# Gates from float32 one-hots with one product a token, and three more gathered rows in flight

## The chip, the cores and the metric

The kernel runs on one core of one Trainium2 chip. The metric is device time in microseconds (us) from launch to end, the median of several runs. Engines are named as in the profile: PE (TensorE matmul; PEld its weight loads), DVE (VectorE), ACT (ScalarE), POOL (GpSimd), SP (SyncE, which issues most DMAs here).

## The reference, cut to what matters

Two layers of a decoder over 512 tokens of width 1024. Each layer is a token mixer (two kinds of attention) with a norm, then a product-key expert layer ("PEER") with a norm. The expert layer is what the change touches:

```
scores = q . sub_keys                 # 8 heads, two halves of 128 keys
top 16 of each half -> sums -> top 16 of the sums:  idx (expert number, 0..16383), gate = softmax
u = expert_u[idx]; act = gelu(h . u)            # 128 selected experts a token, float32
v = expert_v[idx]; y = sum over selected of (gate * act) * v
```

So every token picks 128 of 16384 experts, each with a row of 1024 float32 in `expert_u` and one in `expert_v`.

## The kernel before, in words

The 512 tokens are four blocks of 128. Blocks 0 and 1 (`BLK_A`) take the rows of their experts by **gathering**: `gathers` (L611) fetches, for each of the 128 picks of a token, one row per token with an indirect DMA on POOL's queue (L624, 128 rows of 4 KB at a time), and DVE multiplies and sums it against h (L634, first 128 fetches, from `expert_u`) or adds it, weighted, to y (L643/L645, the next 128, from `expert_v`). A fetch lands in a tile of the pool `gat` (5 buffers of 4 KB a partition), and POOL may issue a fetch when a buffer of that pool is free, that is when DVE is done with an older row. There are 256 fetches for a block and 1024 in all; the four blocks of two layers take turns, one after the other.

Blocks 2 and 3 (`BLK_B`) are **dense**: `dense` (L754) multiplies h with all experts, in 32 chunks of 512 columns, weights the result with a dense matrix of gates, and multiplies that with `expert_v`. Weights stream from HBM; most products are made from high and low parts split by ACT (L748) and DVE (L750). Seven chunks (L776) may be computed before the gates are there; everything else of `dense` waits for the gates of both blocks (`yield f"gates {l} {b}"`).

`gates` (L657) makes that dense matrix and writes it to DRAM (`gdram`). It first calls `select` (L541), the top-16 search on DVE (with products on POOL, L582). Then expert number e is split into i = e >> 7 and j = e & 127, these and the gate are transposed so that a partition holds one of the 128 picks and a column one token (L675), and for each token the matrix G[j, i] = sum over picks of onehot_j x (onehot_i x gate) is one PE product. This goes in 32 steps of NT = 4 tokens a block. A step of the kernel before has, in bfloat16:

- two one-hots of 512 elements (`hots`, L688): on DVE as one comparison against `iota_b` (L700), or on ACT in five instructions (L696, L698)
- the gate is held as three bfloat16 parts that sum to it exactly, so there are three weighted one-hots (L711 on POOL or DVE, L709 on ACT in four instructions)
- `products` (L717): for each token three accumulating matmuls 128x128x128 (L723), and two ACT copies out of PSUM (L727) into a staging tile, which SP writes to DRAM every 32 tokens (L731).

Which engine makes a one-hot or a weighted one is the choice of `pick`, which takes the engine that would end first by a plan kept in the program: `free` holds the planned time at which each engine is next free, and each step tells its planned cost before it emits its instructions (`yield cost(lat=0.7, ACT=0.55, PE=0.8)` for a step of gates, to which `pick` adds; `pace` for a fetched row: DVE 1.14 or 1.2, POOL 1.04, DMA 1.46). All parts of the kernel are generators of that kind, and `run_threads` (L110) runs next the one that the plan can start first (a few us of lead decide between near ones). A step's planned start becomes the priority of its instructions; the framework then orders each engine's queue by priority among what its own timeline holds ready, and adds all waits. On the chip each queue runs in that fixed order.

Tiles of 2 KB a partition come from the pool `d2p` (18 buffers): the one-hots and weights of gates, but also tiles of attention (L270 to L273, L322), of `select`, of the query products (L510) and the split halves of `weigh` (L806, L807). Two more constants matter: `iota_b` holds 0..127 four times over, in bfloat16.

Of the kernel before, what the change touches and what calls it, by code (L numbers as in the profile page):

```python
# [18 lines left out]
P = 128  # L19
# [16 lines left out]
# Pairs (a, b) of ranks that can be among the 16 best sums: (a + 1) * (b + 1) <= 16.  # L36
ROWS = [(0, 1, 16), (1, 1, 8), (2, 1, 5), (3, 1, 4), (4, 1, 3), (5, 3, 2), (8, 8, 1)]
NCAND = sum(n * m for _, n, m in ROWS)
# Token blocks whose experts are gathered row by row (A); the others (B) go through
# products with all experts, in chunks of EC, weighted by a dense matrix of gates.  # L40
BLK_A = [0, 1]
BLK_B = [2, 3]
EC = 512
# [9 lines left out]
def trunk(ctx: ExitStack, tc: tile.TileContext, x, w_in, lam, subln_g, w_o, ln1, ln2,  # L53
# [10 lines left out]
    gat = ctx.enter_context(tc.tile_pool(name="gat", bufs=5))  # L64
    d2p = ctx.enter_context(tc.tile_pool(name="d2p", bufs=18))
# [26 lines left out]
    # The order of the instructions. Threads are generators that tell, before each step that  # L92
    # they emit, how long it will hold the engines; the step that can start first is next.
# [7 lines left out]
    def pick(**engines):  # L101
        """The engine that would end a piece of work first."""
        eng = min(engines, key=lambda e: free[e] + engines[e])
        free[eng] += engines[eng]
        return eng
# [33 lines left out]
    # constants  # L139
    ident = const.tile([P, P], F32, name="ident")  # L140
    make_identity(nc, ident)
    # minus the distance of a query from a key; no weight where the key is later
# [18 lines left out]
    iota_b = const.tile([P, P, NT], BF16, name="iota_b")  # L161
    nc.gpsimd.iota(iota_b, pattern=[[1, P], [0, NT]], base=0, channel_multiplier=0,
# [4 lines left out]
    hs = {}          # a block's h: an SBUF tile (A) or an AP in DRAM (B)  # L167
# [7 lines left out]
    def load_h(b):  # L175
        """A block's h in SBUF, in a tile that may be overwritten."""
        if b in on_chip:
            return hs[b]
        t = hap.tile([P, D], F32, name="ha") if b in BLK_A else t4()
        nc.sync.dma_start(t, hs[b])  # L180
        if b in BLK_A:
            hs[b] = t
            on_chip.add(b)
        return t
# [32 lines left out]
    def layer_params(l):  # L217
        p = {}
        lamt = a2()[:, :4 * HD].rearrange("p (a b) -> p a b", a=4)
        nc.sync.dma_start(lamt.rearrange("p a b -> p (a b)"), rows(lam[l], 4 * HD))  # L220
        tmp = a2()
        s2 = sml.tile([P, 2], F32, name="lam_s")
        for i in range(2):
            nc.vector.scalar_tensor_tensor(tmp[:, :HD], lamt[:, 2 * i, :], 1.0, lamt[:, 2 * i + 1, :],
                                           op0=ALU.mult, op1=ALU.mult, accum_out=s2[:, i:i + 1])
        e2 = sml.tile([P, 2], F32, name="lam_e")
        nc.scalar.activation(e2, s2, AF.Exp)
        li = 0.8 - 0.6 * math.exp(-0.3 * l)
        p["nlam"] = prm.tile([P, 1], F32, name="nlam")
        # -(e1 - e2 + li)  # L230
        nc.vector.scalar_tensor_tensor(p["nlam"], e2[:, 1:2], -li, e2[:, 0:1],
                                       op0=ALU.add, op1=ALU.subtract)
        p["sub_g"] = prm.tile([P, VD], F32, name="sub_g")
        nc.sync.dma_start(p["sub_g"], rows(subln_g[l], VD))
        nc.vector.tensor_scalar_mul(p["sub_g"], p["sub_g"], 1.0 - li)
        LP[l] = p
# [12 lines left out]
    def pipeline(items, stages, skew, c):  # L249
        """Emits the stages of each item, stage k of an item skew[k] steps behind its first."""  # L250
        n = len(items)
        state = [None] * n
        for i in range(n + skew[-1]):
            yield c
            for k, stage in sorted(zip(skew, stages), key=lambda x: -x[0]):
                if 0 <= i - k < n:
                    state[i - k] = stage(items[i - k], state[i - k])

    def attention(l, b, q, mixT):
        """mixT[feature, t] of a block from its queries and all keys up to it."""  # L260
# [135 lines left out]
        # heads of one parity share a tile: the others' keys lie on other partitions  # L396
# [17 lines left out]
    def mixer(l, blks, order, tails):  # L414
        """Token mixer and first norm of some blocks, and their queries and key scores."""
# [9 lines left out]
        # dq dk dv sq sk sv  # L425
        for n, key in ((1, "dk"), (2, "dv"), (0, "dq"), (4, "sk"), (5, "sv"), (3, "sq")):
            o = int(key[0] == "s")
            for b in blks:
# [12 lines left out]
                else:  # L441
# [6 lines left out]
                    else:  # L448
                        # scores in units of the head's slope, a power of two
# [18 lines left out]
    def mixer_out(l, tail, hq):  # L468
# [49 lines left out]
        for b in tail:  # L518
            if b in BLK_B:
                # exact parts of h for the products with all experts  # L520
                HT[b] = hq[b][0]
                xlo, xhi = HQ[b] = [fold(t4(F32R), DC) for _ in range(2)]
                nc.scalar.activation(xhi, hq[b][0], AF.Copy)
                nc.vector.tensor_tensor(xlo, hq[b][0], xhi.bitcast(F32), op=ALU.subtract)
            done[f"scores {l} {b}"] = clock[0]

    def best16(rows, val, pos):
        """The 16 largest of each row, and their positions; the rows are overwritten."""
# [12 lines left out]
    def select(l, b, half, idf, gate):  # L541
        """Expert numbers (as floats) and gates of half of a block's heads: [t, head, rank]."""
# [31 lines left out]
        for h in range(HH + 1):  # L574
            yield cost(DVE=1.35, POOL=1.9)
            if h < HH:
                # a one at the position of each rank, times the expert's number
# [33 lines left out]
    def gathers(l, b):  # L611
        """y = sum over the selected experts of gate * gelu(h . u) * v, rows gathered."""
# [44 lines left out]
    def gates(l, b):  # L657
        """Dense gates of a block to DRAM: gdram[l][j, t // GT, i, t % GT] of expert i * 128 + j."""
# [7 lines left out]
        yield cost(lat=3.0, DVE=2.0, PE=0.7)  # L666
# [9 lines left out]
        t0, t1 = a2(), a2()  # L676
        gp, ij = fold(t0[:, :3 * P], 3), fold(t0[:, 3 * P:].bitcast(BF16), 2)
        ijf, gb = fold(t1[:, :2 * P], 2), fold(t1[:, 2 * P:2 * P + 3 * P // 2].bitcast(BF16), 3)
        nc.vector.tensor_copy(ij.rearrange("p a t -> p (a t)"), pt[:, 0:2 * P])
        nc.scalar.copy(ijf.rearrange("p a t -> p (a t)"), pt[:, 0:2 * P])  # L680
        # three parts of a gate, exact in bfloat16
        nc.vector.tensor_copy(gp[:, 0, :], pt[:, 2 * P:3 * P])
        for k in range(3):
            nc.vector.tensor_copy(gb[:, k, :], gp[:, k, :])
            if k < 2:
                nc.vector.tensor_sub(gp[:, k + 1, :], gp[:, k, :], gb[:, k, :])
                nc.vector.tensor_copy(gp[:, k, :], gb[:, k, :])
        shp = [P, P, NT]  # L688

        def hots(tg, t0):  # L690
            t = tg * GT + t0
            hot = a2h().rearrange("p (a j t) -> p a j t", a=2, t=NT)
            for n in range(2):
                if pick(ACT=1.7, DVE=0.34) == "ACT":
                    for k in range(NT):
                        nc.scalar.activation(hot[:, n, :, k], iota_b[:, :, k], AF.Abs, scale=-1.0,  # L696
                                             bias=ijf[:, n, t + k:t + k + 1])
                    nc.scalar.activation(hot[:, n], hot[:, n], AF.Relu, scale=-1.0, bias=1.0)  # L698
                else:
                    nc.vector.tensor_tensor(hot[:, n], iota_b, ij[:, n, t:t + NT].unsqueeze(1).to_broadcast(shp),  # L700
                                            op=ALU.is_equal)
            w01 = a2h().rearrange("p (a j t) -> p a j t", a=2, t=NT)
            w2 = a2h()[:, :P * NT].rearrange("p (j t) -> p j t", t=NT)
            ws = (w01[:, 0], w01[:, 1], w2)
            for k, w in enumerate(ws):
                eng = pick(ACT=1.2, POOL=1.0, DVE=0.34)
                if eng == "ACT":
                    for n in range(NT):
                        nc.scalar.activation(w[:, :, n], hot[:, 0, :, n], AF.Copy, scale=gp[:, k, t + n:t + n + 1])  # L709
                else:  # L710
                    (nc.gpsimd if eng == "POOL" else nc.vector).tensor_tensor(  # L711
                        w, hot[:, 0], gb[:, k, t:t + NT].unsqueeze(1).to_broadcast(shp), op=ALU.mult)
            return hot, ws
# [3 lines left out]
        def products(tg, t0, hot, ws):  # L717
# [3 lines left out]
            for n in range(NT):  # L721
                for k, w in enumerate(ws):
                    nc.tensor.matmul(ps[:, n * P:(n + 1) * P], lhsT=hot[:, 1, :, n], rhs=w[:, :, n],  # L723
                                     start=(k == 0), stop=(k == 2))
# [10 lines left out]
        for t in range(0, P, NT):  # L735
            yield cost(lat=0.7, ACT=0.55, PE=0.8)
            todo.append((t // GT, t % GT, *hots(t // GT, t % GT)))
# [5 lines left out]
    def split(raw):  # L743
        """Exact halves, hi and lo, of a tile's two parts."""
# [9 lines left out]
    def dense(l):  # L754
        """y of the B blocks from products with all experts."""
# [4 lines left out]
        def first(ec):  # L760
            """gelu(h . u) of a chunk."""
# [29 lines left out]
        def weigh(ec):  # L791
            """Transposed, times the gates, in exact halves."""
# [124 lines left out]
```

## Time and profile before

| | us |
|---|---|
| median of 3 runs (3537.52 to 3541.9) | 3537.8 |
| span of the profiled execution, first to last instruction | 3535.5 |
| DVE busy | 2937.8 (83%) |
| PE busy | 2765.6 (78%) |
| POOL busy | 1681.0 (48%) |
| ACT busy | 1184.8 (34%) |
| DMA, mean rate | 292 GB/s |

No time of the profiled execution other than its span is shown; the median of the runs is 2.3 us above that span. Busy times are unions of an engine's instructions. The stretches of a layer can be told by the lines that run in them. In layer 0: projections until some 300 us; attention of blocks 1 to 3 until some 500; then selections, the gates of block 2 (608 to 784), the query products of blocks 1 and 3, the gates of block 3 (956 to 1089), and from 1110 to 1821 the dense products. Layer 1 repeats this with its gates at 2364 to 2533 and 2703 to 2837, and dense products from 2850 to 3513. The gathered rows run beside all of it, from 167 to 1767 and from 1904 to 3519.

### The profile page before, as it was taken

The numbers are of one execution on the slowest core, as the hardware profiler recorded it, in microseconds if no ns is written. First come the engines' busy times: TensorE is split into PE (matmuls) and PEld (weight loads), VectorE is DVE, ScalarE is ACT, GpSimd is POOL, SyncE is SP. The second block draws the span as 40 slices with busy tenths as digits, with TensorE's granted clock in tenths as the row PEclk, the third lists the DMA queues.
The fourth block names the chain that finished last, engine by engine and source line by source line (L and its number), as shares of the span: only waits on it lengthen the run. The fifth ranks groups of instructions, "written<-read, shape, count | busy, mean of one in ns | idle before, by whom it ended". The sixth has DMA issues, their size and how long they took to land.

```text
span 3535.5 us, 42200 instructions
## 1 busy us (share of the span) xinstructions
PE 2765.6 (78%) x14604; PEld 2214.2 (63%) x14604; DVE 2937.8 (83%) x5537; ACT 1184.8 (34%) x1900; POOL 1681.0 (48%) x1297
## 2 busy tenths in 40 slices
PE   7996474468576999999997876834694679999997
PEld 5776462366245888888776764613652468888885
DVE  2577889989998888888668678999799987888888
ACT  2114640411133444444231138404110434444442
POOL 0265645763675433334314655457536743344443
PEclk9997587579777999999998886865796689999998
DMA  5698796686769999999966987955966799999996
GB/s 228 212 329 294 246 333 201 206 302 231 261 222 360 360 347 343 349 351 348 369 222 253 331 286 237 351 177 196 337 220 232 256 367 343 349 346 354 345 344 251
DMA packets 283926, 1032.89 MB, mean 292 GB/s; under 512 B 25152, under 2 KB 91200, under 8 KB 231488
## 3 DMA queue, kind: packets, MB, share of 16 engines
q0 software_dynamic: 147456, 536.94, 42.4%
q1 hardware_dynamic: 136256, 493.26, 37.6%
q8 instruction: 115, 1.88, 0.2%
q14 instruction: 99, 0.81, 0.1%
HBM read 991.30 MB, written 38.80 MB: 291 GB/s over the span
## 4 chain that ended last, share of the span: by engine, by line
PE 40%; DVE 14%; issue 6%; DMA 5%; POOL 2%; ACT 2%; POOLq 0%; DVEq 0%; ACTq 0%
PE ps L822 7%; PE ps L821 7%; PE ps L824 6%; PE ps L786 5%; PE ps L785 5%; PE ps L784 5%; DVE row L634 3%; DMA row<-u,idx 2%; DVE ha L645 2%; POOL row L624 2%; DMA row<-v,idx 2%; PE ps L800 1%; DVE d L711 1%; DVE idf L586 1%; DVE d L579 1%
## 5 line engine op out<-in xcount | busy, mean ns | idle before, releaser
L624 POOL DMA_INDIRECT row<-v,idx x512 | 669.3, 1307 | 892.6 <-DVE ha L645 662.5
L624 POOL DMA_INDIRECT row<-u,idx x512 | 655.2, 1280 | 589.1 <-DVE row L634 375.9
L634 DVE SCALAR_TENSOR_TENSOR row<-row,ha 128x1024 f32<-128x1024 f32 x512 | 666.6, 1315 | 121.0 <-DMA row<-u,idx 118.1
L645 DVE SCALAR_TENSOR_TENSOR ha<-row,c,ha 128x1024 f32<-128x1024 f32 x508 | 700.3, 1379 | 58.0 <-DMA row<-v,idx 53.9
L750 DVE TENSOR_TENSOR t<-st,t 128x1024 fp32r<-128x1024 f32 x449 | 533.2, 1224 | 210.8 <-ACT t L748 210.7
L748 ACT ACTIVATE t<-st 128x1024 fp32r<-128x1024 f32 x456 | 453.9, 1056 | 36.6 <-PE ps L824 15.8
L723 PE MATMUL ps<-d,d 128*128 128x128 bf16 x1536 | 218.4, 295 | 207.0 <-DVE d L711 128.8
L821 PE MATMUL ps<-t,d 128*128 128x512 f32 x1024 | 314.2, 398 | 44.5 <-ACT d L806 44.5
L822 PE MATMUL ps<-t,d 128*128 128x512 f32 x1024 | 342.3, 395 | 0.0
L723 PEld LDWEIGHTS <-d 128*128 128x128 bf16 x1536 | 178.6, 121 | 234.5 <-issue 192.5
L824 PE MATMUL ps<-t,d 128*128 128x512 f32 x1024 | 316.7, 390 | 0.0
L785 PE MATMUL ps<-t,t 128*128 128x512 f32 x800 | 311.5, 389 | 0.5 <-DVE t L750 0.5
L786 PE MATMUL ps<-t,t 128*128 128x512 f32 x800 | 311.7, 390 | 0.0
L784 PE MATMUL ps<-t,t 128*128 128x512 f32 x800 | 304.2, 389 | 1.0 <-ACT t L748 1.0
L507 PE MATMUL ps<-t,st 128*128 128x128 f32 x2048 | 263.2, 293 | 35.2 <-DMA st<-w_query 35.2
L507 PEld LDWEIGHTS ps<-t,st 128*128 128x128 f32 x2048 | 257.8, 209 | 41.5 <-issue 29.5
L444 PE MATMUL ps<-t,st 128*128 128x128 f32 x2048 | 243.0, 281 | 22.2 <-ACT t L191 16.2
L444 PEld LDWEIGHTS ps<-t,st 128*128 128x128 f32 x2048 | 238.9, 197 | 28.6 <-ACT t L191 18.6
L821 PEld LDWEIGHTS ps<-t,d 128*128 128x128 f32 x1024 | 190.4, 190 | 82.4 <-ACT d L806 45.5
L822 PEld LDWEIGHTS ps<-t,d 128*128 128x128 f32 x1024 | 190.1, 190 | 47.0 <-DVE t L750 10.2
L824 PEld LDWEIGHTS ps<-t,d 128*128 128x128 f32 x1024 | 192.2, 188 | 40.9 <-DVE d L807 0.3
L806 ACT ACTIVATE d<-t 128x512 fp32r<-128x512 f32 x128 | 78.7, 632 | 410.9 <-DVE t L803 410.9
(175 smaller groups left out, 4190.8 us busy)
## 6 DMA issues: line engine op xcount, KB each, us to landing
st<-ut SPq DMA_DIRECT2D x128, 1024.0 KB
st<-vd SPq DMA_DIRECT2D x128, 1024.0 KB
st<-w_in SPq DMA_DIRECT2D x48, 1024.0 KB
st<-w_query SPq DMA_DIRECT2D x48, 1024.0 KB
gd<-st SPq DMA_DIRECT2D x32, 1024.0 KB
t<-gd SPq DMA_DIRECT2D x64, 512.0 KB
st<-w_o SPq DMA_DIRECT2D x24, 1024.0 KB
ln<-ln SPq DMA_DIRECT2D x16, 512.0 KB
```

Source lines behind the costliest of these rows:

```text
L444: nc.tensor.matmul(ps[:, f * P:(f + 1) * P], lhsT=w(c, slice(f * P, (f + 1) * P)), rhs=hT[:, c, :], start=(c == 0), stop=(c == DC - 1))
L507: nc.tensor.matmul(ps[:, f * P:(f + 1) * P], lhsT=w(c, slice(f * P, (f + 1) * P)), rhs=hq[b][0][:, c, :], start=(c == 0), stop=(c == DC - 1))
L624: nc.gpsimd.indirect_dma_start(out=g, out_offset=None, in_=src, in_offset=bass.IndirectOffsetOnAxis(ap=idx[s // (NSEL // 2)][:, s % (NSEL ...
L634: nc.vector.scalar_tensor_tensor(g, g, 1.0, h1, op0=ALU.mult, op1=ALU.mult, accum_out=c[:, s:s + 1])
L645: nc.vector.scalar_tensor_tensor(y, g, c[:, s:s + 1], y, op0=ALU.mult, op1=ALU.add)
L750: (nc.gpsimd if eng == "POOL" else nc.vector).tensor_tensor(lo, part, hi.bitcast(F32), op=ALU.subtract)
L784: nc.tensor.matmul(ap[b], lhsT=xhi, rhs=hi[:, c, :], start=(d == 0), stop=False)
L785: nc.tensor.matmul(ap[b], lhsT=xhi, rhs=lo[:, c, :], start=False, stop=False)
L786: nc.tensor.matmul(ap[b], lhsT=xlo, rhs=hi[:, c, :], start=False, stop=(d == DC - 1))
L821: nc.tensor.matmul(y[b][n], lhsT=shi, rhs=hi[:, n, :], start=start, stop=False)
L822: nc.tensor.matmul(y[b][n], lhsT=shi, rhs=lo[:, n, :], start=False, stop=False)
L824: nc.tensor.matmul(y[b][n], lhsT=slo, rhs=hi[:, n, :], start=False, stop=stop)
```

## The change

`gates` makes float32 one-hots, all on DVE, one instruction for one token and one one-hot, and one product a token; the gate is no longer split. `d2p` goes from 18 to 14 buffers, `gat` from 5 to 8. Comments are dropped too. The core of the diff:

```diff
-    gat = ctx.enter_context(tc.tile_pool(name="gat", bufs=5))
-    d2p = ctx.enter_context(tc.tile_pool(name="d2p", bufs=18))
+    gat = ctx.enter_context(tc.tile_pool(name="gat", bufs=8))
+    d2p = ctx.enter_context(tc.tile_pool(name="d2p", bufs=14))
...
-    iota_b = const.tile([P, P, NT], BF16, name="iota_b")
-    nc.gpsimd.iota(iota_b, pattern=[[1, P], [0, NT]], base=0, channel_multiplier=0,
+    iota_b = const.tile([P, P], F32, name="iota_b")
+    nc.gpsimd.iota(iota_b, pattern=[[1, P]], base=0, channel_multiplier=0,
...
-        yield cost(lat=3.0, DVE=2.0, PE=0.7)
+        yield cost(lat=3.0, DVE=1.2, PE=0.7, ACT=0.4)
...
-        t0, t1 = a2(), a2()
-        gp, ij = fold(t0[:, :3 * P], 3), fold(t0[:, 3 * P:].bitcast(BF16), 2)
-        ijf, gb = fold(t1[:, :2 * P], 2), fold(t1[:, 2 * P:2 * P + 3 * P // 2].bitcast(BF16), 3)
-        nc.vector.tensor_copy(ij.rearrange("p a t -> p (a t)"), pt[:, 0:2 * P])
-        nc.scalar.copy(ijf.rearrange("p a t -> p (a t)"), pt[:, 0:2 * P])
-        nc.vector.tensor_copy(gp[:, 0, :], pt[:, 2 * P:3 * P])
-        for k in range(3):
-            nc.vector.tensor_copy(gb[:, k, :], gp[:, k, :])
-            if k < 2:
-                nc.vector.tensor_sub(gp[:, k + 1, :], gp[:, k, :], gb[:, k, :])
-                nc.vector.tensor_copy(gp[:, k, :], gb[:, k, :])
...
+        ijg = fold(a2()[:, :3 * P], 3)
+        nc.scalar.copy(ijg.rearrange("p a t -> p (a t)"), pt[:, :3 * P])
+
+        def hots(t):
+            hot, w = (fold(a2(), NT) for _ in range(2))
+            for k in range(NT):
+                nc.vector.tensor_scalar(hot[:, k, :], iota_b, ijg[:, 1, t + k:t + k + 1], None, op0=ALU.is_equal)
+                nc.vector.tensor_scalar(w[:, k, :], iota_b, ijg[:, 0, t + k:t + k + 1],
+                                        ijg[:, 2, t + k:t + k + 1], op0=ALU.is_equal, op1=ALU.mult)
+            return hot, w
...
             for n in range(NT):
-                for k, w in enumerate(ws):
-                    nc.tensor.matmul(ps[:, n * P:(n + 1) * P], lhsT=hot[:, 1, :, n], rhs=w[:, :, n],
-                                     start=(k == 0), stop=(k == 2))
+                nc.tensor.matmul(ps[:, n * P:(n + 1) * P], lhsT=hot[:, n, :], rhs=w[:, n, :],
+                                 start=True, stop=True)
...
-            yield cost(lat=0.7, ACT=0.55, PE=0.8)
+            yield cost(lat=1.6, DVE=1.6, ACT=0.9, PE=1.0)
```

The old `hots`, with its two uses of `pick`, goes whole. The copies out of PSUM (L727) and the writes to DRAM (L731) stay.

## Rows read from the trace of the kernel before

**Rows 1.** Gates stretches: start:end, length, PE, PEld, DVE, ACT, POOL, clock, DMA, GB/s.
```profile
608.00:784.00 176.00, 95.22 (x618) 80.91 (x619) 162.10 (x183) 54.73 (x122) 127.41 (x107) 0.64 0.72 250
956.00:1089.00 133.00, 89.58 (x467) 62.01 (x467) 126.77 (x214) 45.41 (x95) 98.63 (x82) 0.69 0.71 252
2364.00:2533.00 169.00, 91.89 (x586) 76.99 (x587) 151.13 (x175) 53.37 (x121) 121.04 (x102) 0.62 0.71 244
2703.00:2837.00 134.00, 88.46 (x467) 61.33 (x467) 125.47 (x214) 44.97 (x95) 100.97 (x83) 0.71 0.70 250
```
**Rows 2.** The same view: between the gates of layer 0, and its dense stretch.
```profile
784.00:956.00 172.00, 119.12 (x539) 78.94 (x539) 164.02 (x583) 21.07 (x32) 76.28 (x59) 0.86 0.68 246
...
1110.00:1800.00 690.00, 683.68 (x3235) 562.97 (x3234) 559.07 (x624) 297.21 (x381) 266.74 (x183) 1.00 0.93 349
```
**Rows 3.** Groups of instructions, whole trace: the lines that go (busy, mean ns, idle before).
```profile
L700 DVE TENSOR_TENSOR d<-iota_b,d 128x512 bf16<-128x512 bf16 x245 | 130.2, 569 | 0.0
L711 DVE TENSOR_TENSOR d<-d,d 128x512 bf16<-128x512 bf16 x195 | 123.6, 662 | 0.1
L711 POOL TENSOR_TENSOR d<-d,d 128x512 bf16<-128x512 bf16 x166 | 196.7, 1197 | 26.8 <-DVE d L700 23.4 <-PE ps L776 1.1 <-PE ps L723 0.5
```
**Rows 4.** Groups of DVE, the gathered rows alone, in the four gates stretches in order.
```profile
L645 DVE SCALAR_TENSOR_TENSOR ha<-row,c,ha 128x1024 f32<-128x1024 f32 x62 | 100.1, 1615 | 13.8 <-DMA row<-v,idx 13.0 <-issue 0.2
...
L634 DVE SCALAR_TENSOR_TENSOR row<-row,ha 128x1024 f32<-128x1024 f32 x45 | 66.5, 1498 | 6.2 <-DMA row<-u,idx 6.2
...
L645 DVE SCALAR_TENSOR_TENSOR ha<-row,c,ha 128x1024 f32<-128x1024 f32 x55 | 90.6, 1647 | 17.9 <-DMA row<-v,idx 17.0
...
L634 DVE SCALAR_TENSOR_TENSOR row<-row,ha 128x1024 f32<-128x1024 f32 x45 | 64.6, 1458 | 8.5 <-DMA row<-u,idx 8.5
```
**Rows 5.** Instructions of one line, whole trace (ns min/median/max): rows and small DVE operations.
```profile
L645 DVE SCALAR_TENSOR_TENSOR ha<-row,c,ha x508: 1224/1280/4344, 455.9 to 3517.6; 128x1024 f32<-128x1024 f32 x170
L634 DVE SCALAR_TENSOR_TENSOR row<-row,ha x512: 1192/1219/7499, 167.5 to 3048.1; 128x1024 f32<-128x1024 f32 x171
L296 DVE TENSOR_SCALAR dg<-ident,rc x64: 260/280/471, 45.1 to 2212.3; 128x128 f32<-128x128 f32 x64
L643 DVE TENSOR_SCALAR ha<-row,c x4: 745/747/754, 453.6 to 3052.9; 128x1024 f32<-128x1024 f32 x4
L205 DVE TENSOR_SCALAR t<-t,ln_mv,ln_rs x8: 802/814/874, 477.2 to 3523.2; 128x1024 f32<-128x1024 f32 x8
```
**Rows 6.** Timeline of DVE, then of POOL, 2399 to 2405 (start us, us).
```profile
2399.79 4.88 DVE L205 TENSOR_SCALAR ha<-ha,ln_mv,ln_rs 128x1024 f32<-128x1024 f32 x1
...
2400.08 4.03 POOL L711 TENSOR_TENSOR d<-d,d 128x512 bf16<-128x512 bf16 x4
```
**Rows 7.** Timeline of DVE, then of POOL, 405.5 to 407.8.
```profile
406.86 0.28 DVE L296 TENSOR_SCALAR dg<-ident,rc 128x128 f32<-128x128 f32 x1
407.06 1.22 DVE L634 SCALAR_TENSOR_TENSOR row<-row,ha 128x1024 f32<-128x1024 f32 x1
...
405.97 1.51 POOL L624 DMA_INDIRECT row<-u,idx  x1 [0.30 <-issue]
```
**Rows 8.** Groups of PE and ACT, whole trace: float32 products 128x128, and a d2 tile's first write.
```profile
L507 PE MATMUL ps<-t,st 128*128 128x128 f32 x2048 | 263.2, 293 | 35.2 <-DMA st<-w_query 35.2
...
L330 ACT ACTIVATE d<-ps 128x512 f32<-128x512 f32 (+1 forms) x44 | 23.9, 548 | 18.9 <-PE ps L328 18.9
```
**Rows 9.** Waits, whole trace (who <- for whom: us, times, longest us).
```profile
POOL row L624 <- DVE ha L645: 662.5, 273, 15.4
DVE row L634 <- DMA row<-u,idx: 118.1, 84, 4.5
DVE ha L645 <- DMA row<-v,idx: 53.9, 39, 4.2
```
**Rows 10.** Waits of DVE for fetched rows, 0 to 300 and then 1800 to 2050.
```profile
DVE row L634 <- DMA row<-u,idx: 28.9, 21, 4.5
...
DVE row L634 <- DMA row<-u,idx: 35.4, 25, 4.1
```

More of the change, by code (lines that the diff above doesn't have):

```diff
@@ L688, in gates @@
[L688 to L704, printed above, removed]
-            for k, w in enumerate(ws):
[L706 to L713, printed above, removed]
@@ L715, in gates, with products @@
         stg = {}
-        def products(tg, t0, hot, ws):
+        def products(tg, t0, hot, w):
             if t0 == 0:
@@ L721, in products @@
             for n in range(NT):
-                for k, w in enumerate(ws):
-                    nc.tensor.matmul(ps[:, n * P:(n + 1) * P], lhsT=hot[:, 1, :, n], rhs=w[:, :, n],
-                                     start=(k == 0), stop=(k == 2))
+                nc.tensor.matmul(ps[:, n * P:(n + 1) * P], lhsT=hot[:, n, :], rhs=w[:, n, :],
+                                 start=True, stop=True)
             ps = fold(ps, NT)
@@ L735, in gates @@
         for t in range(0, P, NT):
-            yield cost(lat=0.7, ACT=0.55, PE=0.8)
-            todo.append((t // GT, t % GT, *hots(t // GT, t % GT)))
+            yield cost(lat=1.6, DVE=1.6, ACT=0.9, PE=1.0)
+            todo.append((t // GT, t % GT, *hots(t)))
             if len(todo) > 1:
```

## The prediction, made before the changed kernel was run

> **What bounds the kernel now.** I read the busy shares first, then the engines by stretch, then the groups of the busiest engine there, and last what its instructions stood against. Over the whole span DVE is the busiest, but the whole-span share mixes stages. In a dense stretch PE is busy 684 of 690 us and the DMA engines 0.93 of the time, while DVE has 131 us to spare [rows 2]. In the four gates stretches, 612 us together, it is the other way round: DVE 565 us, PE 365, ACT 198, POOL 448, DMA 0.7 [rows 1]. Between the two gates of layer 0 DVE is busy 164 of 172 us [rows 2], so time that DVE saves in the first one is not waited away; work queues up behind it until the dense products may begin. The gates stretches are DVE's, and the reader should see what DVE does in them: 254 us are the one-hots and their weighted copies [rows 3], and nearly all the rest gathered rows, 207 of them, 322 us by their groups [rows 4].
>
> The next thing to see is that these instructions are too long. A row takes 1.28 us (L645) or 1.22 us (L634) in the median of the trace [rows 5], but 1.62, 1.50, 1.65 and 1.46 us on average in the gates stretches [rows 4]. L700 and L711 on DVE have means of 0.57 and 0.66 us, with no idle time before them [rows 3]. One place shows who holds them: L205, whose median is 0.81 us [rows 5], took 4.88 us at 2399.8, and for 4.03 us of these POOL ran four L711 products in a row [rows 6]. DVE's instruction ended when POOL's last did. So 166 products on POOL (197 us, rows 3) are not free help: while they run, DVE stands still inside its own instruction, and the profile counts that as busy.
>
> **The change part by part.** The sum is made against the profiled span, 3535.5 us; the median of the runs lies 2.3 us above it and the same is added at the end.
>
> *One-hots on DVE.* Gone: 253.8 us of L700 and L711 [rows 3]. Added: 32 steps x 4 blocks x 8 instructions = 1024 float32 TENSOR_SCALARs of 128 elements. The nearest row is L296, the same form with one scalar from memory: 0.28 us, but the next instruction begins 0.20 us after it (406.86 to 407.06) [rows 5, 7], so 0.20 for the one-hot. The weighted one has two scalars; at 1024 elements the second costs 814 - 747 = 67 ns (L205 against L643) [rows 5], so 0.27. A step is 4 x 0.47 = 1.88 us, 128 steps 241 us. Ends: 205 if the second scalar is free, 322 if durations do not overlap at all (512 x 0.63). I take 241, by the row of the same shape, and add 15 for disturbance: L296 goes up to 0.47 at most [rows 5], and one in twelve stretched by that 0.19 makes 16. Net +2 us: DVE's own work does not shrink.
>
> *Three-part gates.* Some nine small casts, copies and subtractions a block go, at L296's 0.28 about 10 us for four blocks; one ACT copy replaces them. -10 (ends 0 and -15).
>
> *POOL's products.* All 197 us go, and the stalls with them. For rows: 62 x (1.615 - 1.280) + 45 x (1.498 - 1.219) + 55 x (1.647 - 1.280) + 45 x (1.458 - 1.219) = 21 + 13 + 20 + 11 = 64 us [rows 4, 5], and 4 for L205 [rows 6]. -68. Ends: 0, if the fetches on POOL and not its products hold DVE, and -68. A fetch beside L296 did not hold it at all [rows 7], so I take -68.
>
> *PE and ACT.* 1536 bfloat16 products become 512 in float32. With L507's mean of 0.29 us [rows 8] that is 150 us at most; PE idles 247 us in the stretches now [rows 1] and loses more work than it gains. ACT loses its share of one-hots and keeps L727. Counted as nothing. Were the cover gone, a step's four products, 1.2 us, would still be under DVE's 1.9.
>
> *Eight rows in flight.* POOL waits 662 us for DVE to release rows of the second half [rows 9]: with five buffers fetches start late. DVE waits 172 us for rows that have not landed, at most 4.5 us at a time [rows 9]; three more rows in flight are 3.7 us or more of DVE work. In the gates stretches these waits are 13.0 + 6.2 + 17.0 + 8.5 = 45 us [rows 4]; I take 27 of them (ends 0 and 45), since some fetches start late for other reasons, such as their place in POOL's queue. Some 64 us lie in the two projection stretches [rows 10], which PE sets: nothing. Of the remaining 63 us I take 20 (ends 0 and 63).
>
> *Four fewer d2 tiles.* Gates needs two tiles a step instead of three, so it loses little. Attention has no such relief. Where an attention tile is first written, ACT waits for nothing but PE's scores (19 us in all, rows 8), not for a free tile, so there was slack at 18. I take +10 (from 0 to the rival below).
>
> *The plan.* A step's declared DVE time rises from (245 + 195) x 0.34 / 128 = 1.17 us [counts of rows 3] to 1.6: 128 x 0.43 = 55 us, or 46 rows that the plan moves out of the gates stretches and into the dense ones. A row is 0.5 MB, 1.5 us at 349 GB/s, and 7% of 690 us there is room for 32 rows a layer [rows 2]; 23 come. If that room can't be used, 46 x 1.5 = 69 us. I take +15.
>
> Sum: +2 - 10 - 68 - 27 = -103 in the gates stretches (612 to about 509), -20 elsewhere, +10 +15: -98. 3535.5 - 98 + 2.3 = **3440 us**.
>
> **A rule that speaks against it.** In rows 7 a fetch runs on POOL from 405.97 to 407.48, and an L296 that starts in the middle of it is done at 407.14 in its median time, 0.34 us before the fetch's end. The Trainium skill (SBUF — State Buffer, Who interferes with whom) would have the later of the two blocked until the other ends: it counts float32 `tensor_scalar` among the DVE instructions that can run in a two-port mode, and says that these and GpSimd shut each other out for a whole instruction, a GpSimd DMA's descriptor writing included. This case disagrees with that rule; but there are 64 such instructions now, mostly single, and the change puts eight in a row, so the shut-out stays as the third rival.
>
> **The rivals.**
>
> *More rows in flight are the larger part.* All waits for rows outside the projections go, 45 + 63 us, and neither d2 nor the plan costs anything: +2 - 10 - 68 - 108 = -184, 3354 us. For it: POOL's 662 us of waiting for buffers. Against: POOL's queue is in a fixed order, and waits of 1 to 4 us can come from a loaded DMA as well.
>
> *Only half passes on.* The rows, taking turns, run almost to the end of each layer beside the dense products. If what they lose to gates (the plan's 46 rows) or the bound of PE and DMA takes back half of the saving, 3489 us. For it: in the dense stretch DMA has only 7% left. Against: rows follow the same order, and DVE has time there.
>
> *Fetches are shut out by the new instructions.* If a fetch that becomes due in a run of eight TENSOR_SCALARs waits for its end, half of 207 fetches wait half a run, 104 x 0.94 = 97 us; uncovered, this eats the gain: 3537 us, no change. For it: some thousand such instructions where there were 64. Against: rows 7, and eight buffers.
>
> *Slower: attention runs out of d2 tiles.* Its pipeline keeps two tiles a head over four stages (8), and two a pair of units over about three (6), beside query tiles and a selection. If more than 14 are live, attention is throttled to 14/18 of its depth: in its 450 us (300 to 500 and 2050 to 2300) that is 450 x (18/14 - 1) = 129 us, against the gain of 108 without the +10: +21, 3559 us. It decides once more than four tiles' worth of slack is missing there; below 108 us of loss the kernel stays faster. Against: rows 8.
>
> **How the numbers follow.** The forecast has 0.50, more rows in flight 0.17, half 0.16, shut-out fetches 0.07, d2 0.10. The forecast's own range is 3390 to 3485 (its terms' ends for row waits, plan and one-hots). The range leaves out the d2 case and half of the most favourable one: 3345 to 3525. What can be told from no change is 0.2%, 7 us. Faster takes the first three and a quarter of the fourth, 0.84; same 0.05; slower 0.11.
>
> **What would show it.** Right: no POOL product in the gates stretches; L645 and L634 there back to means of 1.3 and 1.25 us; 1024 new instructions with starts 0.20 to 0.27 us apart and some 250 us busy; the four stretches sum to 480 to 530 us if they keep about 200 rows (if they hold few rows they are much shorter, and the dense stretches longer); DVE's waits for rows under 110 us. Wrong: rows still at 1.5 us on average (then fetches hold DVE); new instructions at 0.4 us or more apart (the price, or shut out by fetches); fetches well over 1.3 us on average there; new waits on d2 in attention, or dense stretches that run on after their PE work for the sake of late rows.

## The result, and the profile after

The changed kernel takes 3425.2 us (median of four runs, 3418.7 to 3433.3) against 3537.7 us before (median of four, 3535.7 to 3541.9): ratio 0.968, 95% interval 0.966 to 0.971. The profiled execution has a span of 3428.4 us, 107 us less than before. The head of its page, with the GB/s of 40 slices of the span:

```profile
span 3428.4 us, 41213 instructions
PE 2749.1 (80%) x14092; PEld 2176.0 (63%) x14092; DVE 2848.3 (83%) x6083; ACT 1148.9 (34%) x1760; POOL 1488.2 (43%) x1133
GB/s 235 195 373 285 308 314 236 265 322 277 207 240 388 388 388 391 394 394 262 222 185 235 371 324 234 263 295 227 301 297 242 255 384 393 393 393 393 393 239 150
```

The gates and dense stretches of layer 0, then the gates of layer 1, in the columns of [rows 1]; these lines answer to [rows 1, 2]:

```profile
608.00:803.00 195.00, 136.66 (x888) 119.60 (x889) 181.26 (x494) 46.41 (x87) 74.41 (x66) 0.81 0.72 267
936.00:1003.00 67.00, 57.66 (x273) 41.40 (x272) 67.00 (x273) 36.79 (x68) 9.46 (x7) 0.93 0.51 193
1003.00:1300.00 297.00, 265.96 (x1180) 215.60 (x1181) 262.83 (x338) 116.87 (x140) 163.11 (x110) 0.95 1.01 388
1300.00:1600.00 300.00, 290.09 (x1299) 234.91 (x1298) 278.35 (x264) 124.56 (x148) 141.92 (x96) 1.00 0.98 373
1600.00:1765.00 165.00, 160.88 (x852) 131.23 (x851) 69.31 (x109) 58.73 (x98) 18.44 (x8) 1.00 0.59 219
...
2340.00:2508.00 168.00, 120.53 (x838) 109.78 (x839) 155.16 (x428) 41.30 (x79) 60.64 (x53) 0.82 0.73 276
2640.00:2710.00 70.00, 58.26 (x275) 41.68 (x275) 70.00 (x279) 36.66 (x68) 13.80 (x11) 0.91 0.56 212
```

The second gates stretch of each layer shrank by half (133 and 134 us to 67 and 70); DVE is busy in all of it and POOL in hardly any. The first one did not shrink: of its 494 DVE instructions (183 before) 256 are the new one-hots and 63 are rows, and most of the rest belong to a selection that before stood between the two. The granted clock of PE is higher in these stretches than before (0.81 and 0.93 for 0.64 and 0.69 in layer 0); PE is busy 294 of 489 us from the first gates product to the first dense one before, and 273 of 401 after, so it is not the engine that fills them, but no run here tests what the clock alone is worth. And the dense stretch now has two parts: while rows run, the DMA engines are full (1.01 and 388 GB/s, where the whole stretch had 0.93 and 349) and PE, whose dense products begin at 1020, is busy 266 of the 280 us from there to 1300, where before it had 293 of 293 (1107 to 1400); when the rows are done, the DMA share falls to 0.59.

The new one-hots and the gathered rows, groups of the whole trace (these answer to [rows 3, 5]), and after them the waits that answer to [rows 9]:

```profile
L645 DVE SCALAR_TENSOR_TENSOR ha<-row,c,ha 128x1024 f32<-128x1024 f32 x508 | 652.6, 1285 | 30.3 <-DMA row<-v,idx 24.3
L634 DVE SCALAR_TENSOR_TENSOR row<-row,ha 128x1024 f32<-128x1024 f32 x512 | 633.5, 1255 | 44.8 <-DMA row<-u,idx 35.0
...
L685 DVE TENSOR_SCALAR d<-iota_b,d 128x128 f32<-128x128 f32 x512 | 184.3, 361 | 0.0
L684 DVE TENSOR_SCALAR d<-iota_b,d 128x128 f32<-128x128 f32 x512 | 150.2, 294 | 0.0
```

```profile
POOL row L624 <- DVE ha L645: 407.2, 234, 6.3
...
DVE row L634 <- DMA row<-u,idx: 35.0, 26, 5.0
...
DVE ha L645 <- DMA row<-v,idx: 24.3, 17, 3.4
```

DVE's waits for fetched rows went from 172 us to 59, POOL's for the release of rows of the second half from 662 to 407. A row's operation is back at its undisturbed length on average (1.285 and 1.255 us). To see where that ended up, the instructions of single lines must be read by their first and last start. A dense product and the second half's row, before (layer 0, layer 1, then the row of layer 1):

```profile
L821 PE MATMUL ps<-t,d x512: 387/389/794, 1107.2 to 1820.1; 128*128 128x512 f32 x171
...
L821 PE MATMUL ps<-t,d x512: 387/389/796, 2856.6 to 3512.5; 128*128 128x512 f32 x171
...
L645 DVE SCALAR_TENSOR_TENSOR ha<-row,c,ha x164: 1267/1281/2455, 2481.9 to 3517.6; 128x1024 f32<-128x1024 f32 x164
```

and after:

```profile
L794 PE MATMUL ps<-t,d x512: 387/389/794, 1020.2 to 1759.4; 128*128 128x512 f32 x171
...
L794 PE MATMUL ps<-t,d x512: 387/389/796, 2726.0 to 3413.0; 128*128 128x512 f32 x171
...
L645 DVE SCALAR_TENSOR_TENSOR ha<-row,c,ha x127: 1273/1281/1290, 1236.3 to 1574.9; 128x1024 f32<-128x1024 f32 x127
...
L645 DVE SCALAR_TENSOR_TENSOR ha<-row,c,ha x127: 1273/1281/1287, 2939.8 to 3277.0; 128x1024 f32<-128x1024 f32 x127
```

Two chains of work lead to the end of the kernel. One is gates, then dense products (PE). The other is the gathered rows (DVE), one block after another. Before, both end together, at 3513 and 3518 us. After, the rows end at 3277 and PE ends the kernel at 3413.

**The span cut at the two chains' marks.** A section called gates runs from the first product of a layer's gates to its first dense product, and a dense one to the end of its last; other work, rows above all, lies in them. From the times of each instruction in the trace, in us, with the number of the 1020 row operations (L634 and L645) that start in it in brackets:

| kernel | to first gates | gates L0 | dense L0 | to gates L1 | gates L1 | dense L1 | to the end |
|---|---|---|---|---|---|---|---|
| before | 618 (183) | 489 (148) | 713 (179) | 553 (190) | 483 (142) | 656 (176) | 23 (2) |
| after | 619 (194) | 401 (116) | 740 (200) | 590 (203) | 376 (108) | 687 (199) | 15 (0) |
| e1, 5 rows | 622 (180) | 405 (115) | 714 (188) | 600 (214) | 402 (111) | 656 (174) | 85 (38) |
| e2, gates only | 625 (180) | 401 (115) | 712 (188) | 597 (214) | 405 (111) | 654 (174) | 86 (38) |
| e3, rows only | 605 (198) | 491 (157) | 737 (155) | 547 (203) | 484 (152) | 679 (155) | 15 (0) |
| e4, no POOL | 622 (184) | 503 (193) | 725 (133) | 554 (194) | 483 (182) | 651 (134) | 15 (0) |
| e13, bf16 on DVE | 620 (184) | 504 (181) | 707 (145) | 564 (194) | 467 (159) | 652 (157) | 15 (0) |
| e6, POOL load | 606 (194) | 448 (114) | 740 (202) | 571 (197) | 446 (114) | 687 (199) | 15 (0) |
| e5, old prices | 610 (194) | 407 (134) | 811 (182) | 507 (210) | 365 (108) | 686 (192) | 15 (0) |
| e8, 6 rows | 623 (181) | 413 (130) | 735 (199) | 584 (193) | 406 (123) | 684 (194) | 16 (0) |

The two gates sections lose 195 us; 107 arrive. 95 are given back in the dense stretches (27 and 31) and between them (37), and start and end save another 7. A row takes 1.28 us of DVE (L645) or 1.22 and 0.08 for reading its accumulator (L634), so 1.29 on average. By that, 66 rows fewer are 85 us of the 195, and the sections without their rows went from 298 and 300 us to 251 and 237: 110 us less.

### The profile page after: what moved, and what is told of

Its sections match the earlier page's. It is cut to its first block, busy times and chain, and to the rows that moved or that the text cites. A ratio compares the mean times of both kernels' runs of the same rounds, so it can differ in the third digit from the quotient of the medians.

```text
span 3428.4 us, 41213 instructions
## 1 busy us (share of the span) xinstructions
PE 2749.1 (80%) x14092; PEld 2176.0 (63%) x14092; DVE 2848.3 (83%) x6083; ACT 1148.9 (34%) x1760; POOL 1488.2 (43%) x1133
## 5 line engine op out<-in xcount | busy, mean ns | idle before, releaser
L624 POOL DMA_INDIRECT row<-v,idx x512 | 681.9, 1332 | 612.9 <-DVE ha L645 407.2
L624 POOL DMA_INDIRECT row<-u,idx x512 | 647.0, 1264 | 623.1 <-DVE row L634 360.4
L645 DVE SCALAR_TENSOR_TENSOR ha<-row,c,ha 128x1024 f32<-128x1024 f32 x508 | 652.6, 1285 | 30.3 <-DMA row<-v,idx 24.3
L634 DVE SCALAR_TENSOR_TENSOR row<-row,ha 128x1024 f32<-128x1024 f32 x512 | 633.5, 1255 | 44.8 <-DMA row<-u,idx 35.0
L721 ACT ACTIVATE t<-st 128x1024 fp32r<-128x1024 f32 x456 | 449.5, 1052 | 72.1 <-PE ps L797 37.4
L507 PE MATMUL ps<-t,st 128*128 128x128 f32 x2048 | 266.2, 293 | 59.2 <-DMA st<-w_query 57.5
L759 PE MATMUL ps<-t,t 128*128 128x512 f32 x800 | 311.7, 390 | 0.0
L758 PE MATMUL ps<-t,t 128*128 128x512 f32 x800 | 311.5, 389 | 0.0
L757 PE MATMUL ps<-t,t 128*128 128x512 f32 x800 | 284.0, 389 | 0.0
L444 PE MATMUL ps<-t,st 128*128 128x128 f32 x2048 | 247.0, 282 | 34.4 <-issue 16.4
L749 PE MATMUL ps<-st,t 128*128 128x512 f32 x448 | 199.9, 604 | 23.6 <-DMA st<-ut 23.6
L762 ACT ACTIVATE t<-ps 128x512 f32<-128x512 f32 x128 | 75.4, 598 | 406.2 <-PE ps L759 354.2
```

Source lines behind the costliest of these rows:

```text
L444: nc.tensor.matmul(ps[:, f * P:(f + 1) * P], lhsT=w(c, slice(f * P, (f + 1) * P)), rhs=hT[:, c, :], start=(c == 0), stop=(c == DC - 1))
L507: nc.tensor.matmul(ps[:, f * P:(f + 1) * P], lhsT=w(c, slice(f * P, (f + 1) * P)), rhs=hq[b][0][:, c, :], start=(c == 0), stop=(c == DC - 1))
L624: nc.gpsimd.indirect_dma_start(out=g, out_offset=None, in_=src, in_offset=bass.IndirectOffsetOnAxis(ap=idx[s // (NSEL // 2)][:, s % (NSEL ...
L634: nc.vector.scalar_tensor_tensor(g, g, 1.0, h1, op0=ALU.mult, op1=ALU.mult, accum_out=c[:, s:s + 1])
L645: nc.vector.scalar_tensor_tensor(y, g, c[:, s:s + 1], y, op0=ALU.mult, op1=ALU.add)
L721: nc.scalar.activation(hi, part, AF.Copy)
```

## The experiments

The letters in the expectations stand for these theories. A: POOL's products held DVE, and taking them away is the gain. B: more rows in flight are the larger part. C: rows that come faster crowd the dense stretch. D: two chains share DVE, and the later one ends the kernel. P: the plan's new prices moved the rows. S: one-hots on DVE alone, in bfloat16, are enough (F: they are not). D was formed on e1, e2 and e3. A time in us beside a ratio is the ratio times 3538.

**Each half alone.** e1 is the changed kernel with five row buffers instead of eight, e2 the same with 18 d2 tiles as before, e3 the old gates with the new buffers.

```
e1, against after:   gat bufs=8 -> 5                 (d2p bufs=14)
e2, against after:   gat bufs=8 -> 5                  d2p bufs=14 -> 18
e3, against before:  gat bufs=5 -> 8                  d2p bufs=18 -> 14
```

> The changed kernel with 5 instead of 8 rows in flight (d2p stays at 14). Theory A (POOL's products held DVE; the three extra rows are the smaller part): the 47 us that the prediction gave to the rows come back, 3465 to 3480 us. Theory B (the extra rows are the larger part): more than half of the 112 us gained goes, 3485 us or more. Theory C (the extra rows crowd the dense stretches, where DMA now runs at 388 GB/s and PE has gaps, and gain nothing): 3425 us or less.

> The new gates alone: 5 rows in flight and 18 d2 tiles, as before. Theory A: as the run with 5 rows and 14 d2 tiles, less at most 10 us, 3455 to 3475 us, and L645 and L634 at means of 1.29 and 1.26 us although no row buffer was added. Theory B: 3485 us or more. If d2 tiles are short at 14, this is over 15 us faster than the run with 14.

> The kernel before with 8 rows in flight and 14 d2 tiles, old gates with POOL's products. Theory A: the rows' part alone, 3490 to 3510 us, and rows in the gates stretches still at 1.5 us and more each. Theory B: 3480 us or less. If the old gates, with three d2 tiles a step, suffer from 14 of them: above 3538 us.

Measured: e1 0.983 (0.981 to 0.985), e2 0.984 (0.982 to 0.986), e3 1.004 (1.002 to 1.006). So the new gates alone bring 1.6 to 1.7%, about 59 us, the buffers alone cost 0.4%, 14 us, and both together bring 3.2%, 112 us: 67 more than the sum of the parts. In e1, the last row of layer 1, its last dense product, and the busy times of the end:

```profile
L645 DVE SCALAR_TENSOR_TENSOR ha<-row,c,ha x145: 1237/1281/3439, 2479.3 to 3473.2; 128x1024 f32<-128x1024 f32 x145
...
L794 PE MATMUL ps<-t,d x512: 388/389/796, 2744.1 to 3400.1; 128*128 128x512 f32 x171
```

```profile
3400.00:3485.00 85.00, 1.15 (x6) 0.61 (x4) 65.23 (x64) 0.00 (x0) 47.58 (x37) 0.53 0.72 249
```

The dense products end 112 us earlier than before, the rows only 44, and for the last 85 us PE has 1.15 us of work. In e3 it is the other way round:

```profile
L821 PE MATMUL ps<-t,d x512: 387/389/796, 2863.1 to 3541.9; 128*128 128x512 f32 x171
...
L645 DVE SCALAR_TENSOR_TENSOR ha<-row,c,ha x150: 1272/1283/2716, 2481.7 to 3294.6; 128x1024 f32<-128x1024 f32 x150
```

The rows end 223 us earlier, the dense products, which were last with them, 29 us later. By the recorded ranges e1 (3477 us) is in A's, e2 (3481) between A's and B's, and e3 (3552) where 14 d2 tiles were to hurt the old gates. But e3's gates sections are as long as before; what it loses lies in its dense stretches. Theory D fits all three: each half shortens one chain, and alone it leaves the other as the end. B falls as a theory of its own, since without the new gates the buffers bring nothing. With the new gates and five rows, the difference between e1 and e2 (0.1%, intervals that overlap) is all that four d2 tiles are worth.

**Why the dense stretch grows with more rows in flight.** Bytes and busy share of the DMA queues from 1030 to 1330 us (q0 carries the rows, q1 the loads of the chunks). e2, five rows:

```profile
q1 hardware_dynamic: 23193, 63.12, 55.8%
q0 software_dynamic: 11698, 42.55, 35.9%
```

After, eight rows:

```profile
q1 hardware_dynamic: 21656, 59.03, 52.4%
q0 software_dynamic: 15742, 57.29, 48.5%
```

The rows move 35% more, the chunks for PE 6% less, and the queues together go from 92 to 101% of the engines. Over the 555 us in which rows run beside dense products (1020 to 1575), 6% is some 35 us of loads, of the size of the 23 to 33 us by which every dense stretch with eight rows is longer than its partner with five. PE is idle 25 and 23 us in the dense stretches of the changed kernel, and 7 and 3 in those of e2. The growth goes with the rows in flight and not with the rows in the stretch: e3 has fewer rows in its dense stretches than the kernel before (155 each), and they are 24 and 23 us longer. All this fits theory C, but that the DMA queue is the cause is argued. PE's waits there name the halves that ACT splits (L721, 16 us in 20 waits from 1020 to 1575, and none in e2); only 7 us of ACT's waits before these name a load; and DVE, which shares that work, is busier too (268 us against 245 of the 300).

**POOL's products, taken from the old gates and put back into the new.** e4 is the kernel before without POOL's share of the weighted one-hots. e6 is the changed kernel with one POOL product of the old size a step, whose result nobody reads.

```
e4:  -  eng = pick(ACT=1.2, POOL=1.0, DVE=0.34)
     +  eng = pick(ACT=1.2, DVE=0.34)
e6:  +  load = const.tile([P, 512], BF16, name="load")   # zeros
     ...
     +  j = a2h()[:, :512]
     +  nc.gpsimd.tensor_tensor(j, load, load, op=ALU.mult)   # in each of the 128 steps
```

> The kernel before with one change: the weighted one-hots may go to DVE or ACT, not to POOL. Theory A: DVE gets up to 166 more L711 at 0.34 us (56 us) and loses stalls of 64 us on rows and some 85 us on its own gates work: 3440 to 3480 us, rows in the gates stretches at 1.3 us. Rival (fetches, not POOL's products, hold DVE): rows stay at 1.5 us, and the 56 us come on top: 3560 to 3595 us.

> The changed kernel plus one bfloat16 product of 512 elements on POOL per gates step, 128 in all, whose result nobody reads. Theory A (such products hold DVE inside its own instructions): gates instructions and rows lengthen again by 60 to 120 us in all, all of it in the gates stretches, and since the rows' chain has 135 us to spare it shows as later dense products: 3460 to 3520 us. Rival (POOL's products were harmless for the time, as the run without them was not faster): 3420 to 3440 us.

Measured: e4 1.003 (1.001 to 1.005), e6 0.990 (0.988 to 0.992). In e4 DVE did get its time back (groups of the whole trace; means in [rows 3] were 569 and 662):

```profile
L645 DVE SCALAR_TENSOR_TENSOR ha<-row,c,ha 128x1024 f32<-128x1024 f32 x508 | 653.7, 1287 | 56.4 <-DMA row<-v,idx 54.4 <-DVE ha L645 0.3
...
L711 DVE TENSOR_TENSOR d<-d,d 128x512 bf16<-128x512 bf16 x326 | 122.4, 425 | 1.5 <-ACT d L698 1.3
L700 DVE TENSOR_TENSOR d<-iota_b,d 128x512 bf16<-128x512 bf16 x248 | 93.8, 420 | 0.0
```

Its DVE is 2824.6 us busy instead of 2937.8, although it took over 131 products. The kernel is no faster: 3549 us lies in neither range, though the rows are as theory A had them. The table shows why: the gates sections hold 85 more rows than before (375 against 290). Without their rows they take 254 and 248 us, 96 less than before; the 85 rows put 110 back. The rows came out of the dense stretches, which did not shrink for it, since PE sets them. The stall was real, and its removal went to the chain that was not last.

In e6 the load costs 0.022 of 3538 us, 78 us, and its sections without rows are 301 and 299 us: the value before. The timeline shows how (start, length):

```profile
981.16 0.28 DVE L686 TENSOR_SCALAR d<-iota_b,d 128x128 f32<-128x128 f32 x1
981.27 1.06 POOL L690 TENSOR_TENSOR d<-load 128x512 bf16<-128x512 bf16 x1 [1.47 <-PE ps L700]
981.36 1.06 DVE L687 TENSOR_SCALAR d<-iota_b,d 128x128 f32<-128x128 f32 x1
982.34 0.27 DVE L686 TENSOR_SCALAR d<-iota_b,d 128x128 f32<-128x128 f32 x1
```

The weighted one-hot beside the product takes 1.06 us, as long as the product, instead of 0.34. The second gates stretch went from 59 to 86 us (first to last product) with 32 such products, 0.84 us each. e6 (3504 us) is in theory A's range. Theory A holds for the time of the gates, and does not by itself make a faster kernel.

**One-hots in bfloat16, all on DVE.** If the gain is that gates wait for no other engine, the old bfloat16 one-hots on DVE alone should bring it too. e13 has five rows and 18 d2 tiles, e14 eight and 14.

```
-  if pick(ACT=1.7, DVE=0.34) == "ACT":
+  if pick(DVE=0.34) == "ACT":
...
-  eng = pick(ACT=1.2, POOL=1.0, DVE=0.34)
+  eng = pick(DVE=0.34)
```

> The kernel before, bfloat16 one-hots in three parts and three products a token, 5 rows, 18 d2 tiles, but all five one-hot instructions of a step on DVE and none on ACT or POOL. Theory S (the gates chain gained because a step no longer waits on a leg through POOL or ACT, float32 and the single product do nothing for it): a step is 5 x 0.34 = 1.7 us of DVE, a little less than the new 1.9, so as the new gates alone, 3465 to 3490 us. Theory F (float32 and the single product are needed): 3520 to 3555 us, as the run without POOL.

> The same with 8 rows in flight and 14 d2 tiles. Theory S: as the changed kernel, 3405 to 3440 us. Theory F: 3540 us or more, as the run of the old gates with 8 rows.

Measured: e13 0.997 (0.996 to 0.999), e14 0.996 (0.995 to 0.998). S falls: e13 (3529 us) lies in F's range, e14 (3524) below the 3540 that F gave it. The second gates stretch of layer 0 in e13, and its one-hots in the whole trace:

```profile
970.00:1105.00 135.00, 82.71 (x446) 56.30 (x445) 120.69 (x276) 39.15 (x71) 72.32 (x60) 0.67 0.85 314
```

```profile
L711 DVE TENSOR_TENSOR d<-d,d 128x512 bf16<-128x512 bf16 x384 | 141.8, 422 | 0.0
L700 DVE TENSOR_TENSOR d<-iota_b,d 128x512 bf16<-128x512 bf16 x256 | 96.4, 418 | 0.0
```

640 bfloat16 instructions cost 238 us of DVE, as much as the 1024 in float32 (about 0.45 us a pair, 231 us by their starts). But from its first to its last product this stretch holds 57 rows where the changed kernel's holds 2. The same split runs through all runs: the second gates stretch of layer 0 holds 38 to 70 rows where a token takes three products (before, e3, e4, e13, e14), and 2 to 10 where it takes one (all others), whatever the engines, buffers and prices are. Why the order puts rows between the steps of the one and not of the other is open: the type of the one-hots, the number of products and the d2 tiles of a step changed together in all runs. So F is not shown part by part. In the changed kernel POOL then stands still: of 67 us, it waits 56 for one row to be released, whose operation stands behind the one-hots in DVE's order (group of POOL, 936 to 1003):

```profile
L624 POOL DMA_INDIRECT row<-u,idx x7 | 9.6, 1368 | 57.8 <-DVE row L634 55.9 <-issue 1.2 <-DVE d L685 0.6
```

**The plan's prices.** e5 is the changed kernel with the prices that the plan had before for a step of gates, and for their preparation.

```
-  yield cost(lat=3.0, DVE=1.2, PE=0.7, ACT=0.4)
+  yield cost(lat=3.0, DVE=2.0, PE=0.7)
...
-  yield cost(lat=1.6, DVE=1.6, ACT=0.9, PE=1.0)
+  yield cost(lat=0.7, ACT=0.55, PE=0.8)
```

> The changed kernel with the plan's old prices for gates (a step: lat 0.7, ACT 0.55, PE 0.8, no DVE; preparation DVE 2.0). Theory D (two chains share DVE, gates to dense products and the gathered rows, and the later one ends the kernel): the order hardly hangs on these prices, since the new steps are ready as soon as DVE is; 3415 to 3440 us and the gates of block 3 again with some ten rows. Theory P (it is the new price that gives DVE to gates): rows come back between the steps, 3450 us or more.

Measured: 0.961 (0.960 to 0.963), 3401 us: below both ranges, and faster than both kernels. The two gates stretches of layer 0 in e5:

```profile
600.00:800.00 200.00, 174.34 (x979) 132.59 (x980) 195.56 (x633) 50.86 (x94) 79.83 (x65) 0.93 0.76 285
940.00:1000.00 60.00, 54.37 (x272) 37.99 (x272) 60.00 (x228) 30.79 (x60) 13.31 (x9) 0.97 0.62 237
```

The second stretch, from its first to its last product, holds 10 rows with the old prices, 2 with the new, and is over in 63 us instead of 59. So P falls as the reason why rows left it. The old prices declare nothing for DVE (before, the choice of engine added that), so they are too low here; the first stretch takes 84 us instead of 186 (first to last product), and the sections of e5 differ from the changed kernel's by -9, +6, +71, -83, -11, -1 and 0 us, 27 in all. Which of these made it faster was not told apart.

**How many rows in flight, and at what pace.** e8 and e10 are the changed kernel with six and seven rows; e11 is e5 with seven; e12 is e5 with a row's declared DMA time at 1.9 instead of 1.46.

> The changed kernel with 6 rows in flight. Theory D: with 5 the rows end 75 us after the dense products, with 8 they end 135 us before them; with 6 they end near them, and DMA is less crowded in the dense stretches: 3410 to 3435 us. Theory B (each further row helps by its own): two thirds of the 57 us between 5 and 8 are missing, 3455 to 3470 us.

> The changed kernel with 7 rows in flight. Theory D: rows no longer end last, the dense products do, 3405 to 3425 us, and not slower than with 8. Theory B: 3440 to 3450 us.

> The changed kernel with the plan's old prices for gates (3405 us) and 7 rows in flight. If the rows, which end 150 us before the dense products with 8, crowd DMA while they run: 3390 to 3403 us. If not: 3403 to 3415 us.

> The changed kernel with the old prices for gates, 8 rows in flight, and a row's planned DMA time 1.9 instead of 1.46, so that the plan spreads rows over more of a dense stretch. If the crowded first part of the dense stretches (DMA 388 GB/s, PE idle 30 us in 300) costs time: 3370 to 3400 us. If rows are then late before the next layer: 3410 us or more.

Measured: five to eight rows with the new prices 0.983, 0.977, 0.967, 0.968; e11 0.963 (0.961 to 0.966), e12 0.965 (0.963 to 0.967). The gain of more buffers is over at seven (3420 us, in D's range). Six came out at 3456 us, in B's range and not in D's: the last row starts at 3435 and the last dense product ends at 3444, near each other as D has it, but the dense stretches are already 735 and 684 us long. So D was right on which chain is last, and wrong on the time. e11 (3407 us) and e12 (3413) fell where fewer rows or a slower pace were not to help. In e12 both dense stretches came out shorter than in e5 (754 and 679 us), but the section between the layers and the gates of layer 1 longer (525 and 414), and nothing was left. The higher declared time did not thin out the rows: from 1016 to 1400 us the DMA engines moved 392 GB/s, in e5 394. Of the 30 us in 300 that its expectation gives for PE, 17 lie before the first dense product. So whether the crowding can be turned into time was not tested.

## Why the prediction was right, and where its steps failed

**The time was right: the gates' part on its merits, the rest by luck.** In the prediction's terms, the gates lose 103 us with their rows unchanged, and all the rest adds up to +5 (-20, +10, +15). Measured by the profiled spans, the gates sections without their rows lose 110 (a section also holds the time between its two stretches, so the two figures do not measure quite the same), and all the rest adds up to +3: rows that left the sections -85, dense stretches +58, between them +37, start and end -7. None of these four was in the sum in that size, and that they cancel is luck.

- *One-hots on DVE:* held. The trace has 0.20 us from a one-hot's start to the weighted one's and 0.26 to the next:

```profile
960.07 0.30 DVE L684 TENSOR_SCALAR d<-iota_b,d 128x128 f32<-128x128 f32 x1
960.27 0.36 DVE L685 TENSOR_SCALAR d<-iota_b,d 128x128 f32<-128x128 f32 x1
960.53 0.30 DVE L684 TENSOR_SCALAR d<-iota_b,d 128x128 f32<-128x128 f32 x1
```

  Block 3's 32 steps took 59 us, 1.84 each, for 1.88 predicted.
- *POOL's stalls:* the mechanism held (e4, e6). With five rows (e1, e2) the gates sections without their rows lose 82 and 83 us, where the terms of the gates other than waits, +2 - 10 - 68, make 76. What the prediction did not say is that this saving reaches the end only if the dense products really start earlier. In e4 the sections without their rows lose 96 us, and yet the dense products start 18 us later in layer 0 and 31 in layer 1. One reading was off: L205 did not end with POOL's last product but at 2404.67, 0.56 us after it; its own 0.81 us and the 4.03 make 4.84 of its 4.88, so the 4 us stand.
- *Eight rows in flight:* the size (-47) came out near what e1 and the changed kernel differ by (1.45%, 51 us). The -27 for waits in the gates was good: the sections without their rows are 28 us shorter than in e1. But the dense stretches take back 57, which the sum did not have, and the largest saving is another: the 85 us at the end where, once the new gates are in, DVE works on late rows alone. With eight rows that end is 15 us. With the old gates the same buffers cost 14 us. The prediction treated the terms as independent, and they are not.
- *The plan:* the step that failed. "46 rows that the plan moves out of the gates stretches and into the dense ones ... I take +15": 66 rows left the sections and 44 more lie in the dense stretches, but the sum had only the price of it, and left out the 85 us by which it shortens the sections. The price was wrong as well: with five rows (e1) 64 rows leave the sections, only 7 more lie in the dense stretches, and these are as long as before (714 and 656 us); the 58 us there came with the eight buffers. The sign that was to go with it also failed: the four stretches sum to 484 us from first to last product, inside "480 to 530", but with 118 rows and not 200. And the plan's prices are not what moved the rows (e5); what did is open.
- *d2 tiles:* +10 was nothing with the new gates, and the slower rival with it (e1 against e2).
- *Only half passes on:* in size not far off: of 195 us in the gates sections 88 do not arrive. It did not decide, because the gross saving was larger than thought.
- *Fetches shut out:* refuted. In a run of the new instructions a fetch takes 0.95 us, and they keep their length:

```profile
702.62 0.37 DVE L685 TENSOR_SCALAR d<-iota_b,d 128x128 f32<-128x128 f32 x1
702.73 0.95 POOL L624 DMA_INDIRECT row<-v,idx  x1 [0.30 <-DVE d L685]
702.91 0.28 DVE L684 TENSOR_SCALAR d<-iota_b,d 128x128 f32<-128x128 f32 x1
703.11 0.33 DVE L685 TENSOR_SCALAR d<-iota_b,d 128x128 f32<-128x128 f32 x1
703.36 0.36 DVE L684 TENSOR_SCALAR d<-iota_b,d 128x128 f32<-128x128 f32 x1
```

  28 fetches lie over 70% beside them: mean 0.98 us, at most 1.16, where the mean of all fetches is 1.30 and the median 1.02. What does keep fetches waiting is not the length of the new instructions but DVE's order: the 56 us above, in which no row is released. The Trainium skill (SBUF — State Buffer, Who interferes with whom) would have one of the two wait for the whole of the other; for a fetch this case does not show it. What the section says of a DVE instruction with two SBUF inputs, that it contends with a GpSimd instruction that reads SBUF, agrees with the stalled rows of [rows 4] and e4's mean of 1.287 us.

## What to carry to other kernels

Before adding up savings, find the chains that end a stage or the kernel and say by how much each of two that share an engine is last. Here one half of the change brought 59 us, the other cost 14, and both brought 112. An engine's time that is set free goes to whatever the order puts next on it, and here the order was not understood to the end: e4 freed 113 us of the busiest engine and came out 0.3% slower. When work is displaced, count both what it frees where it was and what it costs where it goes, by counts of instructions in each section of the trace.

## What the runs showed of the hardware that was not expected

- Not only the rows, with two tiles as input, stall, but DVE instructions with a single one too, as L205 in [rows 6]: a float32 TENSOR_SCALAR of 128 elements with two scalars went from 0.34 to 1.06 us beside a POOL product of two SBUF inputs (e6). A fetch that POOL issued beside the same instruction did not stretch it (at most 0.50 us).
- The DMA engines moved 388 to 394 GB/s over slices of 86 us with eight rows in flight, where the dense stretch had 349 before. With five (e2) slices of 7.5 us from 1030 to 1330 reach 424 as well, but about every third moves only 167 to 280.
